# Moving one adaLN vector's row products from VectorE to GpSimd and ScalarE in a decoder layer

## Chip, cores and metric

The kernel runs on one core of one Trainium2 chip. The metric is the device time of one execution in microseconds; the median of the runs counts.

## What is computed

One decoder layer on 256 tokens of width 2048, fp32. The conditioning vector c makes six vectors of 2048, `mod`; the sixth, `gate_f`, is the one whose computation changes.

```python
cs = silu(c)
mod = (cs @ ada_w + ada_b).reshape(6, 2048)
shift_m, scale_m, gate_m, shift_f, scale_f, gate_f = mod
h = rms(x, g0) * (1 + scale_m) + shift_m
# four causal mixers on h @ w_in, each projected and gated by sigmoid(h @ w_gate + b_gate)
x = x + gate_m * rms(mix, g1)
h = rms(x, g2) * (1 + scale_f) + shift_f
a, g = split(h @ ffn_w_in)            # 2048 -> 2 x 5632
x = x + gate_f * rms((silu(a) * g) @ ffn_w_out, g3)
```

## The kernel before

**Matrix products.** Every large weight matrix is read once, as tiles of 128x2048 fp32 (1 MB), by `load` into `raw`, a ring of three buffers (`NR`). SyncE's queue issues the loads. `split` (lines 123 to 148) takes a tile in two halves of 1024 columns: ScalarE casts each half into `whi` (line 137) and VectorE subtracts, `wlo = raw - whi` (the helper of line 75). There are four buffers each of `whi` and `wlo` (`NB`), so two tiles. TensorE then makes three matmuls for each 128 rows of the tile (`mm3t`: high by high, high by low, low by high), first for tokens 0 to 127 and then for 128 to 255, into banks `mmt` of PSUM; that is 24 matmuls of 512 columns for a tile. Activations stand transposed in `hx`, `h2` (in the profile `h`) or `hid`, also split.

**The adaLN vectors.** `ada_w` stands as 6 x 16 tiles of 128x2048. `ada_tile(v, j)` loads one into the same ring `raw`, multiplies it with `cb` (silu of c, the same row in all 128 partitions) and sums along the row into one column of `ada`: one VectorE instruction, `stt` at line 83, which also writes the product over `raw`, and a short read of the accumulator. At j = 15 the bias is added on VectorE. Vectors 0 and 1 are made at the start, 2 to 4 during the mixers. Vector 5 comes last:

```python
todo.extend((5, j) for j in range(NK))
...
for g in range(NJ // 4):
    for s in range(2):
        steps = token_major(A["ffn_in"][g, s], h2, 4, ..., 4 if first else 1, (1, 2, 3))
        for tok, kq in steps:
            ...
            if tok == 1 and kq == 2 and g < 8:
                take_ada(1)
```

So in the first FFN product each of the first sixteen steps (g, s) has four weight tiles W0 to W3, and one ada tile that is loaded after W2 and before W3. Its result is used after the product, in `gate_row(5, 3)`.

**The start of the FFN.** Ahead of it stands the last quarter of the mixers' output product. For each half of the tokens, `mix_out` squares the bank on ScalarE (`sqj`), multiplies it with `gm` into `mixt` on VectorE, and `residual` adds it to `x` and takes the norm: a VectorE and ScalarE chain. `second_norm` scales `mixt`, transposes it on TensorE (line 1002), and makes `hf` and `h`, alternately on ScalarE and VectorE, piece by piece beside the first FFN matmuls.

**Order.** The kernel gives each instruction its engine. A planner then orders each engine's queue by priorities (`high_priority`) and estimated times when the program is built, and gives out the buffers; at run time each engine works its queue in order and waits for what each instruction needs.

Of the kernel before, what the change touches and what calls it, by code (L numbers as in the profile page):

```python
# [13 lines left out]
AF = mybir.ActivationFunctionType  # L14
# [55 lines left out]
def trunk(ctx: ExitStack, tc: tile.TileContext, A: dict, out: bass.AP):  # L70
    nc = tc.nc
    ve, se, te, sy = nc.vector, nc.scalar, nc.tensor, nc.sync

    def tt(o, a, b, op):
        return ve.tensor_tensor(out=o, in0=a, in1=b, op=op)  # L75
# [6 lines left out]
    def stt(o, a, s, b, op0, op1, accum=None):  # L82
        return ve.scalar_tensor_tensor(out=o, in0=a, scalar=s, in1=b, op0=op0, op1=op1, accum_out=accum)  # L83

    def act(o, i, f, bias=None, scale=None, accum=None):
        kw = {}
        if bias is not None:
            kw["bias"] = bias
        if scale is not None:
            kw["scale"] = scale  # L90
        if accum is not None:
            kw["accum_out"] = accum
        return se.activation(out=o, in_=i, func=f, **kw)  # L93
# [4 lines left out]
    MUL, ADD, SUB, MAX, MIN = ALU.mult, ALU.add, ALU.subtract, ALU.max, ALU.min  # L98
# [16 lines left out]
    def load(src, ada=False):  # L115
        if ada and early[0] is not None:
            raw = early[0].tile([P, 2048], F32, name="raw0", tag="raw0", bufs=NA)
        else:
            raw = ring.tile([P, 2048], F32, name="raw", tag="raw", bufs=NR)
        w = src.shape[-1]  # L120
        sy.dma_start(raw[:, :w], src)
        return raw[:, :w]
# [29 lines left out]
    cb = cp.tile([P, D], F32, name="cb")  # L152
# [38 lines left out]
    def ada_tile(v, j):  # L191
        raw = load(A["ada"][v, j], ada=True)
        col = ada[:, v * 16 + j : v * 16 + j + 1]
        stt(raw, raw, 1.0, cb, MUL, MUL, accum=col)
        if v > 1 and j == 15:
            tt(ada[:, v * 16 : v * 16 + 16], ada[:, v * 16 : v * 16 + 16], vp[:, v * 16 : v * 16 + 16], ADD)

# [2 lines left out]
    def take_ada(n):  # L200
        for _ in range(n):
            if todo:
                ada_tile(*todo.pop(0))
# [36 lines left out]
    def chunks():  # L240

        for j in range(NK):
            for v in range(2):
                ada_tile(v, j)
                yield
            x = xq[j // 4][:, j % 4, :]
            tt(ada[:, j : 32 : 16], ada[:, j : 32 : 16], vp[:, j : 32 : 16], ADD)
            t = hxp.tile([P, 512], F32R, name="hx", tag="hx")
            a = amul[:, j : j + 1]
            stt(a, ada[:, 16 + j : 17 + j], 1.0, vp[:, 96 + j : 97 + j], ADD, MUL)  # L250
            act(x, x, AF.Identity, bias=ada[:, j : j + 1], scale=a)
            se.copy(t[:, 0:256], x)
            tt(t[:, 256:512], x, t[:, 0:256].bitcast(F32), SUB)
            hx.append(t)
            yield
# [62 lines left out]
    for r, kr in enumerate(ROUNDS):  # L318
# [3 lines left out]
        if r == 0:  # L322
# [4 lines left out]
            for k in range(kr):  # L327
                need(k)
                raw = load(A["w_lead"][k])
# [925 lines left out]
```

## Time and profile before

| | |
|---|---|
| time, median of 3 runs | 1672.57 us (1669.89 to 1672.8) |
| time of the profiled execution | 1672.82 us |
| its span | 1671.0 us |
| TensorE (PE) busy | 1625.8 us, 97% |
| weight loads of TensorE (PEld) | 1307.9 us, 78% |
| VectorE (DVE) busy | 1190.6 us, 71% |
| ScalarE (ACT) busy | 840.7 us, 50% |
| GpSimd (POOL) busy | 0.2 us, four memsets |
| read from HBM | 398.27 MB |

Times inside the profile are microseconds from the start of the span. A shape is partitions x elements. "Idle before" is the time in which an engine had nothing to do ahead of an instruction, and the arrow names what ended it. Line numbers are those of the kernel before, and a line can be that of a helper: L75 is every `tt`, L83 every `stt`, L93 every `act`, L96 every matmul, L121 every load of `raw`. PE's busy time is modelled from pipelined matmuls. The granted clock is a share of TensorE's full 2.4 GHz.

### The profile page before, as it was taken

To read this page: it belongs to the slowest core of one execution; us is meant where nothing else is said; L and a number is where in the kernel's file an instruction comes from. 1 tells how busy PE (TensorE), PEld (TensorE's weight loads), DVE (VectorE), ACT (ScalarE), POOL (GpSimd) and SP (SyncE) were. 2 spreads that over 40 slices of the span, in tenths; PEclk is the share of its full clock that TensorE was granted. 3 is DMA by queue.
4 is the path that set the end of the run, shared out by engine and by line. 5 is a ranking of instruction groups with operands and counts; after the bars stand their busy time and mean duration, and the time that the engine had idled before them with its cause. 6 is when DMAs were issued, how large, how long until landed. Compare 5 with 4: busy or idle time off the path is not lost.

```text
span 1671.0 us, 19012 instructions
## 1 busy us (share of the span) xinstructions
PE 1625.8 (97%) x7344; PEld 1307.9 (78%) x7344; DVE 1190.6 (71%) x1578; ACT 840.7 (50%) x1135; POOL 0.2 (0%) x4
## 2 busy tenths in 40 slices
PE   5999999999999999999999899999999999999997
PEld 3678888777777777777888688888888888888886
DVE  6689989899899998987656755656565545444444
ACT  3544455678765366365446644444444444444432
POOL 0000000000000000000000000000000000000000
PEclk9999999999999999999999999999999999999999
DMA  9988887775567775775476456666666555655553
GB/s 388 377 317 322 332 336 275 281 261 205 212 210 265 284 264 198 259 264 207 177 254 250 151 201 235 244 238 240 242 229 227 184 200 180 223 184 195 201 185 119
DMA packets 61122, 401.62 MB, mean 240 GB/s; under 512 B 6879, under 2 KB 10468, under 8 KB 13416
## 3 DMA queue, kind: packets, MB, share of 16 engines
q1 hardware_dynamic: 60456, 399.37, 65.4%
q8 instruction: 57, 0.93, 0.2%
q10 hardware_dynamic: 576, 1.05, 0.2%
q14 instruction: 33, 0.27, 0.0%
HBM read 398.27 MB, written 2.12 MB: 240 GB/s over the span
## 4 chain that ended last, share of the span: by engine, by line
PE 83%; DVE 11%; ACT 3%; issue 2%; DMA 1%; SPq 0%; DVEq 0%; ACTq 0%
PE mmt L96 76%; PE mxt L96 4%; DVE wlo L75 3%; PE hs L96 2%; DVE raw L83 1%; ACT whi L137 1%; DVE pc L75 1%; DVE pc L790 1%; DMA raw<-in_w_gate 1%; DVE pq L75 1%; DVE xc L75 1%; ACT L93 1%; PE mxt L1070 1%; PE ys L96 1%; DVE sig L75 1%
## 5 line engine op out<-in xcount | busy, mean ns | idle before, releaser
L75 DVE TENSOR_TENSOR wlo<-raw,whi 128x1024 fp32r<-128x1024 f32 x540 | 652.6, 1217 | 391.9 <-ACT whi L137 376.5
L137 ACT CAST whi<-raw 128x1024 fp32r<-128x1024 f32 x540 | 560.5, 1048 | 578.5 <-PE mmt L96 481.9
L96 PE MATMUL mmt<-whi,hx 128*128 128x512 f32 x1568 | 501.0, 395 | 2.7 <-ACT whi L137 2.6
L96 PE MATMUL mmt<-whi,h 128*128 128x512 f32 x1408 | 439.2, 392 | 1.6 <-DVE h L75 0.8
L96 PEld LDWEIGHTS mmt<-whi,hx 128*128 128x128 f32 x1568 | 294.9, 189 | 70.0 <-issue 6.4
L96 PE MATMUL mmt<-wlo,hx 128*128 128x512 f32 x784 | 308.7, 394 | 4.5 <-DVE wlo L75 4.5
L96 PEld LDWEIGHTS mmt<-whi,h 128*128 128x128 f32 x1408 | 264.5, 188 | 58.6 <-DVE h L75 2.4
L96 PE MATMUL mmt<-wlo,h 128*128 128x512 f32 x704 | 274.4, 390 | 0.0
L83 DVE SCALAR_TENSOR_TENSOR raw<-raw,cb 128x2048 f32<-128x2048 f32 x96 | 218.8, 2283 | 1.9 <-DMA raw<-in_ada 1.6
L96 PE MATMUL mmt<-whi,hid 128*128 128x512 f32 x704 | 217.3, 389 | 0.0
L96 PEld LDWEIGHTS mmt<-wlo,hx 128*128 128x128 f32 x784 | 148.1, 189 | 38.4 <-DVE wlo L75 7.9
L96 PEld LDWEIGHTS mmt<-wlo,h 128*128 128x128 f32 x704 | 132.7, 188 | 27.0
L96 PEld LDWEIGHTS mmt<-whi,hid 128*128 128x128 f32 x704 | 132.1, 188 | 27.4
L96 PE MATMUL mmt<-wlo,hid 128*128 128x512 f32 x352 | 136.9, 389 | 0.0
L96 PE MATMUL mmt<-whi,os 128*128 128x512 f32 x256 | 82.9, 399 | 0.2 <-ACT whi L137 0.2
L96 PE MATMUL mmt<-whi,mx 128*128 128x512 f32 x256 | 79.3, 390 | 0.0
L93 ACT ACT_TABLE_LOAD x58 | 74.4, 1283 | 6.2 <-DVE fx L80 2.9
L96 PEld LDWEIGHTS mmt<-wlo,hid 128*128 128x128 f32 x352 | 66.1, 188 | 13.8
L96 PEld LDWEIGHTS mmt<-whi,os 128*128 128x128 f32 x256 | 48.0, 188 | 13.3 <-ACT whi L137 1.0
L96 PEld LDWEIGHTS mmt<-whi,mx 128*128 128x128 f32 x256 | 48.1, 188 | 9.8
L96 PE MATMUL mmt<-wlo,os 128*128 128x512 f32 x128 | 51.3, 401 | 1.8 <-DVE wlo L75 1.8
L96 PE MATMUL mmt<-wlo,mx 128*128 128x512 f32 x128 | 50.1, 391 | 0.0
(290 smaller groups left out, 1044.0 us busy)
## 6 DMA issues: line engine op xcount, KB each, us to landing
raw<-in_ada SPq DMA_DIRECT2D x96, 1024.0 KB, 5.1
raw<-in_ffn_in SPq DMA_DIRECT2D x88, 1024.0 KB, 5.0
raw<-in_w_gate SPq DMA_DIRECT2D x64, 1024.0 KB, 5.0
raw<-in_ffn_out SPq DMA_DIRECT2D x44, 1024.0 KB, 4.9
raw<-in_w_in SPq DMA_DIRECT2D x40, 1024.0 KB, 6.6
raw<-in_w_branch SPq DMA_DIRECT2D x16, 1024.0 KB, 4.9
raw<-in_w_out SPq DMA_DIRECT2D x16, 1024.0 KB, 4.9
raw<-in_w_lead SPq DMA_DIRECT2D x4, 1024.0 KB, 14.2
```

The lines of the kernel that those rows point to most:

```text
L75: return ve.tensor_tensor(out=o, in0=a, in1=b, op=op)
L83: return ve.scalar_tensor_tensor(out=o, in0=a, scalar=s, in1=b, op0=op0, op1=op1, accum_out=accum)
L93: return se.activation(out=o, in_=i, func=f, **kw)
L96: return te.matmul(o, lhsT=l, rhs=r, start=start, stop=stop, skip_group_check=True)
L137: se.copy(hi[:, :n], s)
L790: ve.tensor_tensor_scan(out=pc[:, c, :], data0=mg, data1=pc[:, c, :], initial=0.0, op0=MUL, op1=ADD)
L1070: te.transpose(ps[:, n * 256 + tok * P : n * 256 + tok * P + P], sa[tok][:, c : c + P], ident)
```

## The change

For v = 5 alone, the product and the row sum become two instructions on two other engines. GpSimd multiplies `raw` by `cb` in place, and ScalarE copies `raw` onto itself and sums the row into the column of `ada`. Loads, order in the program and the vectors 0 to 4 stay as they are.

```diff
     def ada_tile(v, j):
         raw = load(A["ada"][v, j], ada=True)
         col = ada[:, v * 16 + j : v * 16 + j + 1]
-        stt(raw, raw, 1.0, cb, MUL, MUL, accum=col)
+        if v == 5:
+            nc.gpsimd.tensor_tensor(out=raw, in0=raw, in1=cb, op=MUL)
+            act(raw, raw, AF.Copy, accum=col)
+        else:
+            stt(raw, raw, 1.0, cb, MUL, MUL, accum=col)
         if v > 1 and j == 15:
             tt(ada[:, v * 16 : v * 16 + 16], ada[:, v * 16 : v * 16 + 16], vp[:, v * 16 : v * 16 + 16], ADD)
```

## Rows read from the trace of the kernel before

**Rows 1.** The page, part 1: busy us (share) xinstructions by engine.

```profile
...
PE 1625.8 (97%) x7344; PEld 1307.9 (78%) x7344; DVE 1190.6 (71%) x1578; ACT 840.7 (50%) x1135; POOL 0.2 (0%) x4
...
```

**Rows 2.** Windows: span, busy PE PEld DVE ACT POOL, clock, DMA share, GB/s.

```profile
...
916.00:960.00 44.00, 39.74 (x176) 30.65 (x175) 34.78 (x82) 29.58 (x78) 0.00 (x0) 0.92 0.45 165
960.00:1276.00 316.00, 316.00 (x1423) 262.15 (x1422) 187.60 (x172) 134.63 (x142) 0.00 (x0) 1.00 0.64 232
...
```

**Rows 3.** Waits, 960 to 1276: us in total, times, longest.

```profile
...
ACT whi L137 <- PE mmt L96: 166.6, 107, 3.0
...
```

**Rows 4.** Timeline of VectorE, 1085 to 1135: start us, us, what [idle before].

```profile
...
1090.95 1.23 DVE L75 TENSOR_TENSOR wlo<-raw,whi 128x1024 fp32r<-128x1024 f32 x1 [0.62 <-ACT whi L137]
1092.09 2.28 DVE L83 SCALAR_TENSOR_TENSOR raw<-raw,cb 128x2048 f32<-128x2048 f32 x1
...
1094.55 2.58 DVE L75 TENSOR_TENSOR wlo<-raw,whi 128x1024 fp32r<-128x1024 f32 x2 [0.17 <-ACT whi L137]
...
```

**Rows 5.** Timeline of ScalarE, same stretch.

```profile
...
1093.46 1.06 ACT L137 CAST whi<-raw 128x1024 fp32r<-128x1024 f32 x1 [2.54 <-PE mmt L96]
...
1098.90 1.05 ACT L137 CAST whi<-raw 128x1024 fp32r<-128x1024 f32 x1 [3.02 <-PE mmt L96]
...
```

**Rows 6.** SyncE's queue: an ada load's issue, 1086 to 1087.

```profile
...
1086.28 0.33 SPq L121 DMA_DIRECT2D raw<-in_ada  x1
```

**Rows 7.** SyncE's queue: the load after next, 1093 to 1095.

```profile
...
1094.41 0.33 SPq L121 DMA_DIRECT2D raw<-in_ffn_in  x1
```

**Rows 8.** The 16 ada loads: issue to landing.

```profile
...
DMA to landing us min/median/max: 4.8/4.9/5.0
```

**Rows 9.** Groups by shape, 860 to 1400: count, busy us, mean ns, idle before.

```profile
...
L83 DVE SCALAR_TENSOR_TENSOR raw<-raw,cb 128x2048 f32<-128x2048 f32 x16 | 36.5, 2283 | 0.0
...
L93 ACT ACTIVATE sa<-mmt 128x512 f32<-128x512 f32 x21 | 12.6, 598 | 21.5 <-PE mmt L96 21.5
...
L93 ACT ACTIVATION_READ_ACCUMULATOR sqj<-mmt 128x1 f32 x6 | 1.2, 194 | 0.0
...
```

**Rows 10.** Groups by shape: VectorE's scans, whole span.

```profile
...
L790 DVE TENSOR_TENSOR_SCAN pc<-sp,pc 128x256 f32<-128x256 f32 x32 | 20.2, 672 | 0.0
...
```

**Rows 11.** Groups by shape: ScalarE before 860.

```profile
...
L93 ACT ACTIVATE sig<-sig 128x1024 f32<-128x1024 f32 x16 | 17.0, 1062 | 0.2
...
```

**Rows 12.** Timeline of ScalarE, 380 to 412: a Silu, then two Copies.

```profile
...
382.97 1.06 ACT L93 ACTIVATE mlqc<-mlqc 128x1024 f32<-128x1024 f32 x1
...
384.34 0.90 ACT L93 ACTIVATE mlkc<-ml_kT,vp 128x256 f32<-128x256 f32 x2
...
```

**Rows 13.** Chain that ended last, 916 to 945: start us, us, what.

```profile
...
918.21 2.30 DVE wlo L75 x2
...
920.58 2.21 DVE raw L83 x2
...
923.98 0.60 DVE mixt L75
...
937.85 2.21 DVE raw L83 x2
...
940.32 2.12 PE mmt L96 x8
...
```

**Rows 14.** Timeline of ScalarE, 895 to 990.

```profile
...
922.50 0.60 ACT L93 ACTIVATE sqj<-mmt 128x512 f32<-128x512 f32 x1 [1.50 <-PE mmt L96]
...
924.38 1.05 ACT L137 CAST whi<-raw 128x1024 fp32r<-128x1024 f32 x1 [1.19 <-DMA raw<-in_ffn_in]
...
926.46 0.45 ACT L93 ACTIVATE hf<-mxt,ada,amul 128x128 f32<-128x128 f32 x1
...
```

**Rows 15.** TensorE's own waits, 860 to 1400.

```profile
...
PE mxt L1002 <- DVE mixt L79: 2.7, 1, 2.7
...
```

**Rows 16.** Windows: stretches inside the start of the FFN.

```profile
...
926.00:932.00 6.00, 4.60 (x11) 2.35 (x10) 6.00 (x14) 5.65 (x18) 0.00 (x0) 0.50 0.58 232
932.00:940.00 8.00, 8.00 (x41) 6.46 (x39) 7.47 (x20) 3.78 (x12) 0.00 (x0) 0.97 0.37 131
...
```

## The prediction

> **What bounds the kernel now.** I read the page's engine line first: TensorE is busy 97% of the span, VectorE 71%, ScalarE 50%, GpSimd does nothing [rows 1]. A share over the whole span says little of one stage, so I cut out the stage of the change. The sixteen ada tiles of vector 5 lie between 916 and 1276 us, in two different stretches [rows 2]. From 960 to 1276, where fourteen of them lie, TensorE is busy 316.00 of 316.00 us at full granted clock. From 916 to 960, where the first two lie, it is busy 39.74 of 44.00 us, at a clock of 0.92.
>
> In the long stretch the waits show who leads: ScalarE waits 166.6 us, in 107 pieces, for TensorE to give back `whi` buffers [rows 3]. The splitting engines run ahead as far as four buffers (two weight tiles) allow. How far, in time: a ScalarE cast of a first half starts at 1093.46, the next tile's at 1098.90 [rows 5], so TensorE takes 5.44 us for a tile. The cast at 1093.46 starts when TensorE has used that half of the tile two before for the last time, at three quarters of that tile (its token order is half 0, half 1, half 0, half 1). So TensorE wants the new first half 1.36 + 5.44 = 6.80 us later, at 1100.26, and the second half at 1101.62. VectorE has the two low halves ready at 1094.55 + 1.29 = 1095.84 and at 1097.13 [rows 4]. The slack is 4.4 to 4.5 us per tile. This slack is the measure for everything below.
>
> The first 44 us are another matter. The chain that ended last runs there through VectorE almost without a break, and the ada product stands in it twice, 2.21 us each at 920.58 and 937.85 [rows 13].
>
> **What is removed.** Sixteen VectorE products of 2.28 us, 36.5 us in all [rows 9]. In the long stretch, 14 x 2.28 = 32 us go from an engine that has 316.0 - 187.6 = 128 us idle, while TensorE has none [rows 2]: worth nothing. At the start two times 2.21 us go from the chain. The second is worth at most 0.2 us: TensorE was busy 8.00 of 8.00 us while it ran [rows 16]. The first is worth at most its 2.2 us, for TensorE waits 2.7 us for VectorE's `mixt` right behind it [rows 15], and perhaps more: after that wait TensorE is granted 0.50 of its clock (the 1.2 GHz level) for 6 us, in which 4.6 busy us could have been 2.3 [rows 16]. The upper bound of all gain is therefore the 4.26 us idle plus 2.3, some 6.5 us. I don't expect it. VectorE's next step, the product of the last bank with `gm`, follows ScalarE's square of the same bank, which runs 922.50 to 923.10 [rows 14]; VectorE reached it at 923.98 [rows 13]. With the queue's order as it is, 0.7 to 0.9 us come forward. And ScalarE's first `hf`, at 926.46, stands behind a cast that waited for its load until 924.38 [rows 14]. I take a gain of 0.7 us, bounds 0 and 6.5.
>
> **What is added on GpSimd.** Sixteen products of 128x2048, two inputs. This trace has no GpSimd work to price them by. The nearest row is the same product on VectorE, 2.28 us; the slowest streaming row of fp32 is VectorE's scan, 672 ns for 256 elements [rows 10], 2.63 ns each, 5.4 us for 2048. I keep 2.3 to 5.4 and work the sum at 5.4, because only a slow product can hurt. The ada load leaves at 1086.28 [rows 6] and lands 4.9 us later [rows 8], at 1091.2; the product ends between 1093.5 and 1096.6.
>
> The Trainium skill, GPSIMD Engine Reference (Elementwise, side-by-side cycle accounting), gives 4497 ns for this size and dtype and calls GpSimd about half as fast as VectorE; no run here shows it yet. By it the product would end at 1095.7, and the sum below would stay what it is.
>
> **What is added on ScalarE.** Sixteen Copies of 128x2048 with a row sum. From 598 ns for 512 [rows 9] and 1062 for 1024 [rows 11], 2048 make 1062 + 2 x 464 = 1990 ns, and the accumulator read 194 [rows 9]: 2.2 us. A table load of its own is unlikely: two Copies at 384.34 follow the Silu of 382.97 without one [rows 12]. Should each sum bring a pair of 1.28 us loads, it would take 4.7 us, 1.7 more than the 3.02 us that ScalarE idles before 1098.90 [rows 5], inside the slack. What matters is where the sum stands in ScalarE's queue, for everything behind it waits for GpSimd too. That order isn't the program's: the tile W2 is loaded and split before ada's, yet VectorE does the ada product at 1092.09 and W2's `wlo` at 1094.55 [rows 4]. The planner puts a step where its inputs come ready by its estimates. So three places:
> - behind both casts of W2, free from 1095.9: the sum ends at 1096.6 + 2.2 = 1098.8 at the latest, in the gap. Free.
> - between them: the second cast ends at 1099.9, its `wlo` at 1101.2; wanted at 1101.6. Free.
> - ahead of both: first cast 1098.8 to 1099.9, its `wlo` to 1101.2, wanted at 1100.26: 0.9 us late at 5.4; on time at 2.3.
> I take one of the first two: 0 us for fourteen tiles.
>
> At the start ScalarE has 5.65 of 6 us busy from 926 to 932 [rows 16], so a 2.2 us sum there pushes others; it could also fall partly into the 1.19 us idle before 924.38 [rows 14]. I take 1.0 us once, bounds 0 and 4.4 for two.
>
> **The raw slot.** The ring has three. A slot comes back after the sum, 1098.8 at worst, instead of after the product, 1094.4. The load that waited for it left at 1094.41 [rows 7]; its tile is cast at 1098.90 + 5.44 = 1104.3. It would leave 4.4 us late and land at 1103.7 by the 4.9 us of [rows 8], before its cast, and the 4.4 us of slack stand behind that. 0 us. The closing addition of the biases (j = 15) waits on ScalarE now and may hold VectorE once for a few us: inside the slack, 0.
>
> **Sum.** -0.7 + 1.0 + 0 = +0.3 us on the profiled execution's 1672.82, which lies 0.25 above the median of the runs, 1672.57: I say 1673.0.
>
> **The rivals.**
> A, slower: the sums stand ahead of W2's casts and GpSimd is slow. It decides from a product of 4.5 us: 1091.2 + 4.5 + 2.2 + 1.06 + 1.29 = 1100.26. At 5.4 it costs 0.9 us a tile, and 1.8 if the product also starts 0.9 us later, behind VectorE's `wlo` that ends at 1092.1 [rows 4]. Fourteen times: 13 to 25 us, 1686 to 1698. For it: ScalarE idles 2.54 us before 1093.46 [rows 5], an inviting place; against: only an estimate of GpSimd near VectorE's 2.3 would put the sum there.
>
> B, slower: the two engines get in each other's way in SBUF, a product holding up VectorE's two-input steps for its whole length. In the long stretch that is bearable: W2's `wlo` start at 1097.5 at worst (1092.1 + 5.4) and end at 1098.8 and 1100.1, before 1100.26 and 1101.6. At the start it isn't: a product from 920.5 to 925.9 in place of 2.2 us on VectorE costs the chain 3.1 us, the second as much at most: 3 to 6 us, 1676 to 1679. At 2.3 us it would cost nothing, so it decides from about 4.
> The Trainium skill, SBUF (Who interferes with whom), states this: a VectorE instruction with two SBUF inputs contends with a GpSimd instruction that reads SBUF, and the later one waits. `wlo` (raw and `whi`), `x` and `h` are of that form; this trace, without GpSimd work, can't show it.
>
> C, faster: the planner uses VectorE's freed time at the start and brings `mixt` forward by the full 2.2 us, and the clock stays up: 3.5 to 6.5 us, 1666 to 1669. For it: VectorE is the chain there; against: the ScalarE steps above, and the sums, which go to the same place.
>
> **How the numbers follow.** My forecast (within 0.2%, or 3.3 us, which is about what a measurement of this kernel can tell from no change) has 0.52: one stretch has no TensorE idle to win and 4.4 us slack to lose. A has 0.17, B 0.15, C 0.14; 0.02 are for a loss larger than A, such as both stretches failing. Faster 0.14, same 0.52, slower 0.34. The likeliest case alone spans 1670 to 1676. The range takes in B, most of C and the lower end of A: 1667 to 1686 leaves out about half of A, the tip of C and the rest.
>
> **What would show it.** TensorE busy 316 of 316 us in the long stretch: the forecast; gaps of about 1 us at each tile, ended by ScalarE's cast or `wlo`: A. Where the sums stand against W2's casts is read in ScalarE's timeline. `wlo` or `x` far above 1.23 us, or GpSimd far above 4.5, at times when both run: B. TensorE's 2.7 us wait gone, and 926 to 932 at full clock: C. A product over about 7 us, a table load with every sum, or ada loads landing late would make the forecast wrong through the slack.

## The result and the profile after

The changed kernel takes 1690.8 us (median of 4, 1689.85 to 1693.0) beside 1671.94 us before (the three runs of the table above and one more): a ratio of 1.0117, interval [1.0099, 1.0134]. It is 19 us slower; the forecast was 1673 with a range of 1667 to 1686. Beside other runs of the kernel before, the same file took 1688.16 against 1671.15 (last experiment), 1.0092 [1.0074, 1.011].

The engine line of the page and the two stretches of [rows 1, 2], after (us of the stretch; busy PE, PEld, DVE, ACT, POOL; clock; DMA share; GB/s):

```profile
...
PE 1632.7 (97%) x7344; PEld 1307.3 (77%) x7344; DVE 1160.8 (69%) x1546; ACT 866.1 (51%) x1167; POOL 82.7 (5%) x20
...
```

```profile
...
916.00:960.00 44.00, 34.23 (x146) 25.95 (x146) 36.43 (x71) 30.61 (x76) 9.94 (x2) 0.92 0.42 153
960.00:1276.00 316.00, 308.83 (x1366) 251.86 (x1366) 144.47 (x141) 148.93 (x167) 67.19 (x13) 0.99 0.61 216
...
```

VectorE has 30 us less to do, and TensorE has lost its unbroken stretch: 308.83 of 316.00 us where it was 316.00, and 34.23 of 44.00 at the start where it was 39.74. The groups of the two new instructions (count, busy us, mean ns, idle before and what ended it), and the waits from 960 to 1296 that answer to [rows 3]:

```profile
...
L195 POOL TENSOR_TENSOR raw<-raw,cb 128x2048 f32<-128x2048 f32 x16 | 82.5, 5156 | 1210.8 <-DVE wlo L75 918.3 <-DMA raw<-in_ada 235.5 <-DVE sa L75 41.4
...
L93 ACT ACTIVATE raw<-raw 128x2048 f32<-128x2048 f32 x16 | 30.7, 1918 | 89.2 <-POOL raw L195 89.2
...
L93 ACT ACTIVATION_READ_ACCUMULATOR raw<-raw 128x1 f32 x16 | 2.9, 182 | 0.0
...
```

```profile
...
ACT raw L93 <- POOL raw L195: 85.2, 14, 7.9
...
PE mmt L96 <- DVE wlo L75: 6.0, 13, 0.8
...
```

Here is the loss of the long stretch: ScalarE's sum waits 85.2 us for GpSimd, and thirteen times TensorE then waits for a `wlo`. One ada tile on ScalarE, VectorE, TensorE and GpSimd, where [rows 4, 5] showed one before:

```profile
...
1155.90 1.92 ACT L93 ACTIVATE raw<-raw 128x2048 f32<-128x2048 f32 x1 [5.76 <-POOL raw L195]
1157.72 0.18 ACT L93 ACTIVATION_READ_ACCUMULATOR raw<-raw 128x1 f32 x1
1157.81 3.88 ACT L137 CAST whi<-raw 128x1024 fp32r<-128x1024 f32 x4
...
```

```profile
...
1158.88 4.63 DVE L75 TENSOR_TENSOR wlo<-raw,whi 128x1024 fp32r<-128x1024 f32 x4 [7.48 <-ACT whi L137]
```

```profile
...
1158.38 0.62 PE L96 MATMUL mmt<-whi,h 128*128 128x512 f32 x2
...
1159.06 0.61 PE L96 MATMUL mmt<-whi,h 128*128 128x512 f32 x2
1160.16 0.50 PE L96 MATMUL mmt<-wlo,h 128*128 128x512 f32 x1 [0.48 <-DVE wlo L75]
1160.49 0.63 PE L96 MATMUL mmt<-whi,h 128*128 128x512 f32 x2
...
```

```profile
...
918.74 5.41 POOL L195 TENSOR_TENSOR raw<-raw,cb 128x2048 f32<-128x2048 f32 x1 [918.30 <-DVE wlo L75]
939.64 4.53 POOL L195 TENSOR_TENSOR raw<-raw,cb 128x2048 f32<-128x2048 f32 x1 [15.49 <-ACT h L1018]
...
1151.03 4.84 POOL L195 TENSOR_TENSOR raw<-raw,cb 128x2048 f32<-128x2048 f32 x1 [18.71 <-DMA raw<-in_ada]
...
```

The sum stands ahead of all casts of the next tile in ScalarE's queue. GpSimd's product runs from 1151.03 to 1155.87; ScalarE has idled 5.76 us for it, sums until 1157.8, and only then casts four halves in a row, none of which waits for TensorE. TensorE waits 0.48 us for the `wlo` of 1158.88. It loses more than that, because the row counts the wait from the modelled end of a matmul: from 1158.38 to 1159.06 three matmuls start in 0.68 us, and the three from 1159.06 to 1160.49 need 1.43, so 0.75 us are lost at this tile. The 6.0 us of waits above are too small in the same way.

At the start something else happens. The products of 918.74 and 939.64 in the rows above meet these VectorE instructions, and ScalarE's first sum:

```profile
...
917.37 2.38 DVE L75 TENSOR_TENSOR wlo<-raw,whi 128x1024 fp32r<-128x1024 f32 x2
...
920.08 5.15 DVE L75 TENSOR_TENSOR wlo<-raw,whi 128x1024 fp32r<-128x1024 f32 x1 [0.27 <-ACT whi L137]
...
939.67 4.85 DVE L75 TENSOR_TENSOR h<-hf,h 128x128 fp32r<-128x128 f32 x2
...
```

```profile
...
924.18 1.92 ACT L93 ACTIVATE raw<-raw 128x2048 f32<-128x2048 f32 x1 [3.94 <-POOL raw L195]
...
```

A `wlo` that takes 1.23 us [rows 4] is stretched to 5.15 us and ends at 925.23, 1.1 us after the product (924.15). Two `h` subtractions of 128x128, 0.29 us each elsewhere, take 4.85 us together. TensorE's own waits from 860 to 1420, two of them, answer to [rows 15]:

```profile
...
PE mmt L96 <- DVE h L75: 5.2, 3, 3.2
PE mxt L1006 <- DVE mixt L79: 4.2, 1, 4.2
...
```

The wait for `mixt` has grown from 2.7 to 4.2 us and that for `h`, 0.8 us in two pieces before, to 5.2 us in three.

**Where the 19 us lie.** The profiled executions reach the FFN up to 6.3 us apart, for reasons ahead of it, so stretches are compared between three marks of each trace: the first norm's sum (the first 128x1<-128x4 reduction of `st` on VectorE), the fourth and the twentieth `silu` of the FFN on ScalarE (start times). Start is the second mark less the first, over the 87.54 us of the kernel before; long stretch the third less the second, over its 355.57.

```
kernel                         marks (us)                    start   long stretch
before                         912.95  1000.49  1356.06        -          -
the change                     912.19  1007.01  1376.11      +7.28     +13.53
e2  no sum                     909.13  1003.39  1358.75      +6.72      -0.21
e3  from the third tile        910.26   998.80  1364.71      +1.00     +10.34
e4  half the product           912.63  1002.78  1358.35      +2.61      -0.00
e5  late sum, from the third   908.80   996.35  1351.75      +0.01      -0.17
e1  product on VectorE         915.11  1004.62  1359.97      +1.97      -0.22
e8  first two tiles alone      909.99  1003.50  1358.86      +5.97      -0.21
e6  before, one group later    910.55   998.16  1353.52      +0.07      -0.21
e11 late sum, one group later  910.12   997.56  1353.38      -0.10      +0.25
e9  longer product             910.11   999.55  1384.15      +1.90     +29.03
e10 the change again           911.62  1005.78  1371.86      +6.62     +10.51
```

The third ada tile ends before the fourth `silu` in all but e6 and e11, so what it costs (0.7 us in e3) is in "start". The table's parts make 20.8 us and not 19, because the profiled execution of the change took 1693.0 us, 20.2 more than that of the kernel before, and was 0.8 us ahead at the first mark.

### The profile page after: what moved, and what is told of

Same layout as the page of the kernel before. It is cut to its first block, busy times and chain, and to the rows that moved or that the text cites. A ratio compares the mean times of both kernels' runs of the same rounds, so it can differ in the third digit from the quotient of the medians.

```text
span 1691.1 us, 19040 instructions
## 1 busy us (share of the span) xinstructions
PE 1632.7 (97%) x7344; PEld 1307.3 (77%) x7344; DVE 1160.8 (69%) x1546; ACT 866.1 (51%) x1167; POOL 82.7 (5%) x20
## 4 chain that ended last, share of the span: by engine, by line
PE 67%; DVE 16%; DMA 8%; ACT 5%; issue 3%; POOL 0%; SPq 0%; DVEq 0%; ACTq 0%; POOLq 0%
PE mmt L96 61%; DVE wlo L75 7%; DMA raw<-in_ffn_in 4%; PE mxt L96 3%; ACT whi L137 3%; DMA raw<-in_ada 2%; DVE raw L83 2%; DMA raw<-in_w_gate 1%; PE hs L96 1%; DVE pc L75 1%; DVE pc L794 1%; DVE pq L75 1%; DVE xc L75 1%; ACT L93 1%; PE ys L96 1%
## 5 line engine op out<-in xcount | busy, mean ns | idle before, releaser
L75 DVE TENSOR_TENSOR wlo<-raw,whi 128x1024 fp32r<-128x1024 f32 x540 | 653.8, 1224 | 437.7 <-ACT whi L137 426.3
L83 DVE SCALAR_TENSOR_TENSOR raw<-raw,cb 128x2048 f32<-128x2048 f32 x80 | 182.5, 2284 | 2.4 <-DMA raw<-in_ada 2.0
L195 POOL TENSOR_TENSOR raw<-raw,cb 128x2048 f32<-128x2048 f32 x16 | 82.5, 5156 | 1210.8 <-DVE wlo L75 918.3
L93 ACT ACTIVATE raw<-raw 128x2048 f32<-128x2048 f32 x16 | 30.7, 1918 | 89.2 <-POOL raw L195 89.2
```

What stands on the lines that cost most here:

```text
L195: nc.gpsimd.tensor_tensor(out=raw, in0=raw, in1=cb, op=MUL)
```

## The experiments

**e2: the product without the sum.** ScalarE's sum is left out; vector 5 is its bias alone.

```diff
+    ve.memset(ada[:, 80:96], 0.0)
...
             nc.gpsimd.tensor_tensor(out=raw, in0=raw, in1=cb, op=MUL)
-            act(raw, raw, AF.Copy, accum=col)
```

> All sixteen products stay on GpSimd, ScalarE's row sum is left out (vector 5 is its bias alone). Queue theory (the sum stands ahead of two casts in ScalarE's queue and waits there for GpSimd): the long stretch is TensorE 100% busy again, as nothing in ScalarE's queue waits for GpSimd; the start keeps the two VectorE instructions that GpSimd holds up, so 3 to 6 us over the kernel before: 1675 to 1678. Port theory (the product holds up VectorE's splits at every tile and this is the loss): about 1688 to 1691, as the products are all still there. Theory that the sum's own 2.1 us are the loss: 1675 to 1678 too.

Measured: 1676.39 against 1670.41, ratio 1.0032 [1.0017, 1.0047]. Its window of the long stretch, and its `wlo` from 900 to 1300:

```profile
...
960.00:1276.00 316.00, 316.00 (x1424) 262.32 (x1423) 178.44 (x141) 134.18 (x142) 71.85 (x14) 1.00 0.65 229
...
```

```profile
...
L75 DVE TENSOR_TENSOR wlo<-raw,whi 128x1024 fp32r<-128x1024 f32 x134 | 193.1, 1451 | 147.8 <-ACT whi L137 143.4
...
```

TensorE is busy all the time again, although the mean `wlo` is stretched to 1451 ns from 1224 by the products. So products holding up VectorE cost nothing in the long stretch; the slack takes them. The start keeps +6.7 us without any sum, and a `wlo` at 917.03 takes 5.15 us there too: that loss is GpSimd's product against VectorE.

**e3: the change from the third tile on**, and **e8: for the first two alone.**

```diff
-        if v == 5:
+        if v == 5 and j > 1:      # e3; e8 has j < 2
```

> The change from the third ada tile on; the first two stay on VectorE. If the loss is made of two parts, about 6 us at the start and about 13 us in the long stretch (0.75 us at each tile): 1684 to 1687. If it is the start alone: 1671 to 1673. If it is the long stretch alone: 1690.

> The change for the first two ada tiles alone. If the parts add: the start's 6.7 us and nothing else, 1676 to 1679. If the start's loss is taken back in the long stretch, where VectorE and ScalarE have room: 1671 to 1673.

Measured: e3 1681.79 against 1670.41, ratio 1.0066 [1.0047, 1.0085], long stretch +10.3; e8 1675.59 against 1671.26, ratio 1.003 [1.0018, 1.0042], start +6.0, long stretch -0.2. The parts are separate and they add: 0.3% and 0.66% make 0.96%, and the change alone made 0.92% (e10) and 1.17%. e3 came out 2 us under its expectation, which had counted 13 us for the long stretch.

**e4: half the product.** GpSimd multiplies the first 1024 columns; the rest of the row is summed without its factor.

```diff
-            nc.gpsimd.tensor_tensor(out=raw, in0=raw, in1=cb, op=MUL)
+            nc.gpsimd.tensor_tensor(out=raw[:, 0:1024], in0=raw[:, 0:1024], in1=cb[:, 0:1024], op=MUL)
```

> GpSimd multiplies only the first 1024 of the 2048 columns (the rest of the row is summed without the factor); ScalarE's sum is whole and where it was. Queue theory, by which a long product makes the sum late: the product takes about 2.6 us, below the 4.5 us at which a sum ahead of the casts starts to cost, so the long stretch is clean; the start loses 1 to 3 us: 1672 to 1676. Theory that the sum's own 2.1 us on ScalarE are the loss: 1684 or more, since the sums are unchanged.

Measured: 1673.57 against 1670.41, ratio 1.0017 [1.0008, 1.0027]. The product's group (ns min/median/max, first and last start):

```profile
...
L195 POOL TENSOR_TENSOR raw<-raw,cb x16: 2395/3010/3387, 919.1 to 1271.3; 128x1024 f32<-128x1024 f32 x16
...
```

At 3.0 us the long stretch loses nothing, with every sum ahead of the casts as in the change and as long as there (1917 ns): the sum's own 2.1 us are not the loss. The start falls from +7.3 to +2.6 us.

**e5: the sum two casts later.** From the third tile on, each sum gets a bias of zero made of the low half of the tile split before it, so it can't be placed ahead of that tile's casts.

```diff
+            latest[0] = lo        # in split: the last wlo made
...
-        if v == 5:
+        if v == 5 and j > 1:
...
+            z = cp.tile([P, 1], F32, name="zlate")
+            ts(z, latest[0][:, 0:1].bitcast(F32), 0.0, None, MUL)
-            act(raw, raw, AF.Copy, accum=col)
+            act(raw, raw, AF.Identity, bias=z, accum=col)
```

> As the one with the first two tiles on VectorE, but each sum is made to depend on the low half of the tile loaded before it (a bias of zero, made of that half), so that it stands two casts later in ScalarE's queue. Queue theory: products and sums are all there, yet the loss of the long stretch is gone: 1671 to 1674. Port theory, or a loss by the sum's own time: 1684 to 1687, as in the kernel without this dependence.

Measured: 1671.52 against 1670.41, ratio 1.0002 [0.9992, 1.0013]. One tile on ScalarE, VectorE and GpSimd, and the two windows:

```profile
...
1090.63 1.05 ACT L137 CAST whi<-raw 128x1024 fp32r<-128x1024 f32 x1 [0.30 <-PE mmt L96]
1094.97 2.01 ACT L93 ACTIVATE raw<-raw,zlate 128x2048 f32<-128x2048 f32 x1 [3.28 <-DVE zlate L79]
...
1096.97 1.99 ACT L137 CAST whi<-raw 128x1024 fp32r<-128x1024 f32 x2
...
```

```profile
...
1090.36 4.32 DVE L75 TENSOR_TENSOR wlo<-raw,whi 128x1024 fp32r<-128x1024 f32 x2 [2.38 <-ACT whi L137]
...
```

```profile
...
1087.65 4.81 POOL L196 TENSOR_TENSOR raw<-raw,cb 128x2048 f32<-128x2048 f32 x1 [17.99 <-DMA raw<-in_ada]
...
```

```profile
...
916.00:960.00 44.00, 39.54 (x175) 30.87 (x175) 33.09 (x79) 27.81 (x71) 0.00 (x0) 0.92 0.41 144
960.00:1276.00 316.00, 316.00 (x1424) 262.21 (x1423) 182.59 (x157) 159.94 (x170) 69.75 (x14) 1.00 0.66 232
...
```

Product and sum are there, GpSimd as slow as before, and the two `wlo` at 1090.36 take 4.32 us instead of 2.58 because the product runs until 1092.46. Yet TensorE is busy 316.00 of 316.00: the sum now runs behind the casts, at 1094.97. But for one short VectorE step a tile (`zlate`), this is the work of e3 in another order of ScalarE's queue, 10 us faster than e3. The place of the sum is the cause of the long stretch's loss.

**e1: the product back on VectorE**, as a plain multiplication, the sum on ScalarE as in the change.

```diff
-            nc.gpsimd.tensor_tensor(out=raw, in0=raw, in1=cb, op=MUL)
+            tt(raw, raw, cb, MUL)
```

> The product goes back to VectorE as a plain multiplication (2.2 us), the row sum stays on ScalarE; GpSimd does nothing. Theory so far: in the long stretch the sum no longer waits 5 us, TensorE is 100% busy; at the start no GpSimd product holds VectorE up, so the 6.7 us of the start are gone but for what the two sums of 2.1 us push on ScalarE: 1671 to 1674. If the start's loss came from the sums in ScalarE's queue and not from the held-up VectorE steps, the start keeps its 6 to 7 us: 1677.

Measured: 1672.18 against 1671.26, ratio 1.0007 [0.9999, 1.0015]. TensorE's own waits, 860 to 1400:

```profile
...
PE mmt L96 <- ACT h L1018: 4.4, 2, 4.0
PE mxt L1006 <- DVE mixt L79: 2.7, 1, 2.7
```

The long stretch is clean. The start loses 2.0 us: the two sums there push ScalarE's `h`, for which TensorE waits 4.4 us (0.7 before). Without GpSimd 5 of the start's 7 us are gone. (This profiled execution was a long one, 1676.8 us; the medians differ by 0.9 us in all.)

**e6: the kernel before with its ada steps one group later**, so that none lies at the start; and **e11: the same with products on GpSimd and late sums**, for a version that could beat both.

```diff
-                if tok == 1 and kq == 2 and g < 8:
+                if tok == 1 and kq == 2 and 1 <= g < 9:
```

> The kernel before, with all ada products on VectorE, but the sixteen steps begin one group later (groups 1 to 8), so that none lies at the start. Theory: two products of 2.2 us leave VectorE's chain there; the second was covered by TensorE's backlog, the first moves the transposes by 0.7 to 2.2 us: 0.7 to 3 us faster, 1667.5 to 1670 beside 1670.4. If ScalarE and the loads set the start: no change.

> Products on GpSimd and late sums as in the late-sum kernel, for all sixteen tiles, beginning one group later. Both causes of loss are avoided: as fast as the kernel with the shifted steps on VectorE, 1667.5 to 1671. If GpSimd's products still cost in the long stretch: slower than that one by 5 us or more.

Measured: e6 1670.53 against 1671.26, ratio 1.0001 [0.9993, 1.001]; e11 1671.14 against 1671.26, ratio 0.9998 [0.999, 1.0007]. Neither beats the kernel before. TensorE's own waits in e6:

```profile
...
PE mmt L96 <- ACT h L1014: 4.2, 2, 3.1
...
PE mxt L1002 <- DVE mixt L79: 0.3, 1, 0.3
```

The wait for `mixt` fell from 2.7 us to 0.3, and the wait for ScalarE's `h` rose from 0.7 to 4.2. VectorE was freed, and ScalarE's queue, which takes the second token half's squares ahead of that cast, became what TensorE waits for. My expectation of 0.7 to 3 us was wrong; the other branch, no change, held.

**e9: a longer product, from the third tile on.** A further product of 512 columns follows each product (those columns are multiplied by the row twice). In ScalarE's queue as built, the sum stands between the two casts.

```diff
-        if v == 5:
+        if v == 5 and j > 1:
             nc.gpsimd.tensor_tensor(out=raw, in0=raw, in1=cb, op=MUL)
+            nc.gpsimd.tensor_tensor(out=raw[:, 0:512], in0=raw[:, 0:512], in1=cb[:, 0:512], op=MUL)
```

> The change from the third tile on, and GpSimd does a further product of 128x512 after each product (the first 512 columns are multiplied by the row twice). By the order of ScalarE's queue as built, the sum then stands behind the first and ahead of the second of the two casts. GpSimd takes about 1.3 us longer at a tile, but the second half is wanted 1.36 us later than the first: by the arithmetic of the slack the loss a tile stays near 0.75 us, 1680 to 1684, as with the plain change from the third tile on. If each microsecond of product costs a microsecond wherever the sum stands: 0.75 + 1.3 us for fourteen tiles, about 1699. If a place between the casts is free, as the forecast had it for a product up to 5.4 us: 1671 to 1674.

Measured: 1703.84 against 1671.15, ratio 1.0194 [1.0165, 1.0223]; none of the three expected times. GpSimd, VectorE and ScalarE at one tile:

```profile
...
1098.87 5.04 POOL L195 TENSOR_TENSOR raw<-raw,cb 128x2048 f32<-128x2048 f32 x1 [17.12 <-DMA raw<-in_ada]
1104.00 2.15 POOL L196 TENSOR_TENSOR raw<-raw,cb 128x512 f32<-128x512 f32 x1
...
```

```profile
...
1101.82 3.18 DVE L75 TENSOR_TENSOR wlo<-raw,whi 128x1024 fp32r<-128x1024 f32 x1 [2.37 <-ACT whi L137]
...
```

```profile
...
1100.73 1.05 ACT L137 CAST whi<-raw 128x1024 fp32r<-128x1024 f32 x1 [2.54 <-PE mmt L96]
1106.18 1.92 ACT L93 ACTIVATE raw<-raw 128x2048 f32<-128x2048 f32 x1 [4.39 <-POOL raw L196]
...
1108.09 2.93 ACT L137 CAST whi<-raw 128x1024 fp32r<-128x1024 f32 x3
...
```

The 512 columns took 2.15 us, not 1.3: the `wlo` that the first product held up ends at 1105.00, 1.1 us after that product, and the second op, with a quarter of the columns, ends 1.15 us later. So GpSimd is busy about 2.2 us longer at a tile. By the arithmetic of the slack this makes 0.75 + 2.2 - 1.36 = 1.6 us a tile. Where nothing else happens the trace's `silu` shift by 3.29 us for two tiles (from +7.27 to +10.56 against before, 1086.66 to 1131.11), 1.64 each: the thirteen tiles of the long stretch make 21.3 us. The other 7.7 of the 29.0 came in three jumps of 1.6, 3.3 and 2.8 us over that pace. Each falls at a late ada load: from the load's issue to the start of its product it took 7.3, 7.4 and 6.8 us there (issues at 1019.9, 1164.7 and 1215.7), and 5.0 to 5.6 at the other eleven. A place between the casts is therefore not free as such; by this arithmetic it moves the limit by 1.36 us.

**e10: the change again.**

> The change unaltered, beside the same runs of the kernel before. If the parts add: the first two tiles 5 to 6 us, the other fourteen 10 to 12, so 1686 to 1689 beside 1671. If the ada load that landed 7.7 us after its issue and cost 3.8 us belongs to the kernel, it comes again in this profile and the time is 1689 to 1692.

Measured: 1688.16 against 1671.15. Start +6.6, long stretch +10.5, 17.1 in all against 17.0 of the medians. The 3 us more of the first profile are one event: its `silu` shift by 1.5 us for each two tiles, but by 5.27 between 1089.38 and 1131.11. The landing of the ada loads of that first profile has an outlier:

```profile
...
DMA to landing us min/median/max: 4.8/4.9/7.7
```

In [rows 8] the longest was 5.0; in e10 6.3. (In each of these profiles, that of [rows 8] too, the trace has a landing for eight of the sixteen loads only.) The load issued at 1095.79 landed 7.74 us later and the chain that ended last runs through it; it is some 3.8 us of the 13.5. Counted from the issue to the start of the product, which every load has, this one took 7.9 us and the other fifteen 4.9 to 5.5. Late loads came in other profiles too: one of 6.4 us in e10 and one of 6.4 in e3, where the `silu` fell back 0.7 and 0.6 us more than their pace, and, with next to no loss in the long stretch (-0.17 and +0.25), two of 7.1 and 6.6 in e5 and four of 6.1 to 7.4 in e11. What holds such a load up stays open.

## Why the prediction was wrong

**The step that failed** is the end of the part on ScalarE: "I take one of the first two: 0 us for fourteen tiles." The sum stands at the third place, ahead of both casts. The working of that place held: a limit of 4.5 us for the product, and a loss of 0.9 us at 5.4. Measured were products of 5.2 us (median) and 0.75 us a tile; e4 at 3.0 us lost nothing. The text chose between the places without a row for it, although it had named the 2.54 us of idle ahead of the cast as inviting. That the planner puts the sum there because it takes GpSimd's product for shorter than it is was argued, not shown. What e5 shows is that moving the sum alone gives back 10 us.

**The second term that failed** is the start: -0.7 + 1.0 us forecast, +6.0 to +7.3 measured. This is rival B, with its price of 3 to 6 us. e2 (no sum, +6.7) and e1 (no GpSimd, +2.0) show the held-up VectorE steps to be the larger share. Of the two terms that stood there, the 1.0 us for the sums fits e1 (+2.0 in its profile, 0.9 between its medians), and the gain of 0.7 did not show: with both products gone from the start, e6 is at +0.07. The text used 5.4 us for the product in the long stretch, "because only a slow product can hurt", and then left the same 5.4 us out of the start's sum, where VectorE was the chain [rows 13].
By the Trainium skill, SBUF — State Buffer (Who interferes with whom), the later of a two-input VectorE instruction and a GpSimd product waits; the trace agrees, 5.15 us in place of 1.23.

**A and B were treated as two cases** of which one could come, with 0.02 for both. Both follow from the same thing, a product of about 5 us, so together they were likelier than either alone. 0.75 x 14 = 10.5 and the 6.0 of e8 make 16.5, close to the 17 of e10; the range ended at 14 over the median.

**What held.** GpSimd's price lay between 2.3 and 5.4 us: 4.53 at the least, 5.16 on average. By the Trainium skill, GPSIMD Engine Reference (Elementwise), a two-input add of this size takes 4.50 us; the trace agrees where nothing held the product up (4.53 us at 939.64). ScalarE's sum: 1990 + 194 ns forecast, 1918 and 182 measured, and no added table load (58 on the page before and after). VectorE's 32 us in the long stretch were worth nothing. The slack of 4.4 us, in e2 and e5, took products, held-up `wlo` and late slots of the ring at no cost. Rival C is false by e6: with both products gone from the start, TensorE's wait only changes its name.

## What to carry to other kernels

Work moved off a busy engine to an idle one is paid for by whoever waits for it in order: before pricing it, find where the waiting instruction will stand in its queue and compare the wait with the slack there, at the slow end of the price. If one unknown price drives two rivals, add them up. And where an engine is the chain and its work is taken away, look for the wait that is next: here it changed from VectorE's `mixt` to ScalarE's `h` and nothing was gained.

## What the runs showed of the hardware

GpSimd's product of 128x2048 fp32 took 4.53 to 5.41 us in the change, that of 128x1024 2.40 to 3.39 in e4. In the rows shown, VectorE subtractions with both inputs in SBUF that met a running product ended about their own length after the product's end (1.1 us after it for one of 1.23, 2.2 for two of 1.29); a product that started while a `wlo` was running was the longer for it (5.41 us at 918.74, beside a `wlo` until 919.75; 4.53 at 939.64). An ada load landed after a median of 4.8 to 5.2 us in these profiles, but after 7.7, 7.1, 6.3 and 7.2 at the longest in those of the change, of e9, e10 and e11: with slack left such a landing isn't seen (e11), and with the slack used up it shows in the time (3.8 us in the change).
